# New prices per matrix product in the planner that orders TensorE's work in a hybrid decoder step

## The chip, the cores and the metric

One core of one Trainium2 chip. The metric is the device time of one execution in microseconds (us); lower is better. The comparison is of medians over several executions.

## The reference

Two layers of a hybrid decoder, on a prompt of 1024 tokens and on 8 single-token samples with cached state. Each layer projects the normalised input once and feeds three branches, whose gated outputs are joined and projected back:

```python
h = _rmsnorm(x, p['norm_g'], NORM_EPS)
z = h @ p['w_in']
u, g_pool, q, k, v, g_attn, rin, g_rwkv = _split(z, (D_POOL, D_POOL, D_ATTN, D_KV, D_KV, D_ATTN, D_SHIFT, D_RWKV))
a_out, new_pool = _pool_mixer(u, pool_buf, pos0, p['pool_w'], p['pool_scale'])   # windows of 2, 4, 8, 16 tokens
b_out, new_k, new_v = ...      # sliding-window attention (128), rotary, learned sinks
c_out, new_shift, new_wkv = _rwkv_mix(rin, shift_prev, wkv0, p)                  # a recurrence over tokens
mix = jnp.concatenate([a_out * silu(g_pool), b_out * silu(g_attn), c_out * silu(g_rwkv)], axis=-1)
y = x + mix @ p['w_out']
```

The recurrence is the part with a long chain in it; for each token it reads and updates a 64x64 state per head:

```python
sa = jnp.einsum('bhvk,bhk->bhv', S, kk_t)
S = S * w_t[:, :, None, :] - sa[..., None] * (kk_t * a_t)[:, :, None, :] + v_t[..., None] * k_t[:, :, None, :]
o = jnp.einsum('bhvk,bhk->bhv', S, r_t)
```

## The kernel before

**The work.** Tokens lie along the columns: two halves of 520 and 512, the first with the 8 samples in it. A layer's half is `in_half` (21 tiles of 128 output columns of `w_in`) and later `out_half` (8 tiles of `w_out`). Each operand of a projection is split into a high and a low part in a rounded 32-bit type (`hh`, `hl` for the activations, `wh`, `wl` for the weights) and three products are added, wh·hh, wh·hl and wl·hh, over 8 blocks of 128 rows. So a tile is 24 products of 512 columns, or 48 of 256 and 264. These are called products here; they all write a tile named `acc`. Every other matrix multiplication is in plain float32 and is small:

- `rwkv_prep` makes the terms of 256 tokens (a group g, four per layer): `lora`, `kn`, `bonus` twice, then `gram` twice; then a triangular solve on VectorE, then `CA<-cst,xrkv` and `CA<-cst,BK`.
- `rwkv_chain` runs the recurrence over 8 pieces of 32 tokens. A piece is three groups on TensorE, each waiting for the copies of the one before by VectorE and ScalarE: `CA<-XS,AG` (copied into `ys`), `CA<-ys,TZ` (copied into `XS`), `CA<-XS,BT` (copied into `XS` of the next piece). Outputs of the piece before (`CB<-XS,AG`) ride behind the first. After the last piece comes a group norm on `osb` (VectorE and ScalarE), then `back`, 16 small multiplications that turn `osb` around.
- attention: `ps` (scores), softmax, `pt` (transposes), `po` (values). Others: `qn`, `pn`, `pool`, `ssum`, `vtr`.

**What sets the order on TensorE.** The instructions of TensorE stand in one fixed order, chained by `placed` (line 289 on). It is worked out while the program is built, by a planner with a clock of its own, `pe[0]`, in us. Each multiplication adds its price in cycles, divided by 2400 (`pe[0] += cost / 2400.0`). The prices are in `mm` (from line 302) and `transpose`. Products are the background. After each of them `tick` looks at six streams of side work (chain, finishing steps, preparation, three of attention) and runs every step that has come due. When a step is due is worked out in `after`:

```python
least, scale = (MT0, MT1) if job.tight else (job.stream.least, job.stream.scale)
return pe[0] + scale * (at_of(*what) - pe[0]) + least
```

`at_of` is when the planner believes that the step's inputs are ready, from prices of the other engines' instructions. So delays are in us, and how many products lie in such a delay depends on what a product is priced at. Where the products have run out and a job must be finished, `need` moves the clock forward to the next step that comes due, and nothing lies between the steps then.

**The end.** `out_last` does the last half of layer 1. First it runs the products of 6 of the 8 row blocks, 8 tiles of 18 products of 512 columns, with the last chain between them (chain g = 3). Then it needs that chain, with `back` and two steps after it on POOL, and runs the 48 products of the last two row blocks. The orders of the other engines come from the framework's scheduler, which is given TensorE's.

Of the kernel before, what the change touches and what calls it, by code (L numbers as in the profile page):

```python
# [9 lines left out]
F32 = mybir.dt.float32  # L10
# [76 lines left out]
def hybrid_step_kernel(ctx: ExitStack, tc: tile.TileContext, I, O):  # L87
# [17 lines left out]
    def there(ap, at):  # L105
        name = ap.tensor.name
        ready[name] = max(at, ready.get(name, 0.0))
# [183 lines left out]
    def placed(ins, cost, out):  # L291
        if pe[1] is not None:
            tc.add_manual_dep(
                ins.ins, pe[1].name,
                mybir.DependencyInfo(mybir.DependencyClass.NoSync, mybir.DependencyReason.DATA),
                reason="order of the streams",
            )
        pe[1] = ins.ins
        pe[0] += cost / 2400.0
        there(out, pe[0] + 0.1)  # L300

    def mm(out, lhsT, rhs, start=True, stop=True, **kw):
        n = out.free_size()
        if rhs.dtype == F32:
            m = out.shape[0]
            half = m > 64 and lhsT.shape[0] <= 64
            n = max((2.7 if half else 4.2) * n, 500) if m > 64 else max(2.7 * n, 235) if m > 32 else max(1.6 * n + 64, 140)
        else:
            n = max(n, 270)
        placed(T.matmul(out=out, lhsT=lhsT, rhs=rhs, start=start, stop=stop, **kw), n, out)  # L310

    def transpose(out, in_, identity):
# [2 lines left out]
    def flip(out, in_, rows):  # L315

        mm(out=out, lhsT=in_, rhs=ident[rows, rows], start=True, stop=True)
# [68 lines left out]
    def products(w, xs, o, n, acc, k, of=8):  # L386
        wh, wl = w[k // 4]
        xh, xl = xs[0][k]
        for i, (a, b) in enumerate(((wh, xh), (wh, xl), (wl, xh))):
            mm(  # L390
                out=acc[:, :n], lhsT=a[:, k % 4, :], rhs=b[:, o:o + n],
                start=(k == 0 and i == 0), stop=(k == of - 1 and i == 2), skip_group_check=True,
            )
            tick()

    def products_wa(w, xs, o, n, acc, k):
        xh, xl = xs[0][k]
        wk = w[k // 4]
        mm(
            out=acc[:, :n], lhsT=wk[:, k % 4, :], rhs=xh[:, o:o + n], start=(k == 0), stop=(k == 7),  # L400
            skip_group_check=True,
        )
        tick()
        mm(
            out=acc[0:64, :n], lhsT=wk[:, k % 4, 0:64], rhs=xl[:, o:o + n], start=False, stop=(k == 7),
            skip_group_check=True,
        )
        tick()
# [1270 lines left out]
```

## Time and profile before

| | |
|---|---|
| median of 3 runs | 1204.05 us (1202.91 to 1211.36) |
| the profiled execution | 1207.17 us |
| its span, first to last instruction | 1205.4 us |
| TensorE (PE) busy, share of the span | 1100.6 us, 91% |
| VectorE (DVE), ScalarE (ACT), GpSimd (POOL) busy | 876.1, 620.8, 519.0 us |
| mean granted clock of TensorE | 0.953 of full |

A busy TensorE is one with a multiplication in flight. Multiplications are pipelined, so one of them lasts longer than the distance between two starts; that distance, from row to row of a timeline, is what one costs in a stream. A float32 multiplication is two records in the trace, one of the rounded type a single one. The granted clock is 1 at 2.4 GHz and 0.5 at 1.2 GHz.

### The profile page before, as it was taken

Reading aid. Unit: us, or ns where it says so; the run is one execution under the profiler, and the core shown is the slowest. Engines: PE = TensorE matmul, PEld = TensorE weight load, DVE = VectorE, ACT = ScalarE, POOL = GpSimd, SP = SyncE. Lnnn points to the kernel's source line nnn. Section 1 sums busy time; section 2 is a strip of 40 time slices with the busy share of each in tenths; the row PEclk is TensorE's granted clock in tenths of the full one; section 3 lists DMA queues with packets and bytes.
Section 4 is the critical chain, followed back from the end, with each engine's and each line's share of the span. In section 5 each row is a group of like instructions: output and inputs, shape, how many; then the busy total and the mean of one; then the engine's idle time right before and its main releaser. Section 6 shows DMA issues by size and latency. Waiting matters only on the chain.

```text
span 1205.4 us, 24519 instructions
## 1 busy us (share of the span) xinstructions
PE 1100.6 (91%) x9258; PEld 875.0 (73%) x9258; DVE 876.1 (73%) x1783; ACT 620.8 (52%) x1579; POOL 519.0 (43%) x544
## 2 busy tenths in 40 slices
PE   5999889899999898999999879999998889899995
PEld 4998778566766577878998768667676666688764
DVE  6548897668677885877788998896428796787523
ACT  4445454655546563655465536545645444655331
POOL 5156545433455245340364363444445534432441
PEclk8999999799999898999999999999999988999997
DMA  5442224322322134343422322443442121333221
GB/s 172 130 132 79 61 88 125 122 81 99 97 83 72 42 98 124 107 125 112 145 70 73 93 66 63 134 140 112 144 138 81 60 84 50 100 122 118 92 84 73
DMA packets 81234, 120.33 MB, mean 100 GB/s; under 512 B 20430, under 2 KB 30174, under 8 KB 81116
## 3 DMA queue, kind: packets, MB, share of 16 engines
q1 hardware_dynamic: 81116, 118.77, 31.6%
q8 instruction: 72, 1.18, 0.4%
q14 instruction: 46, 0.38, 0.1%
HBM read 94.28 MB, written 19.17 MB: 94 GB/s over the span
## 4 chain that ended last, share of the span: by engine, by line
PE 51%; DVE 30%; DMA 5%; issue 5%; ACT 5%; POOL 3%; SPq 2%; DVEq 0%; POOLq 0%; ACTq 0%
PE acc L310 35%; DVE pr L150 4%; PE CA L310 4%; DVE AG L150 3%; DVE hl L150 2%; PE po L310 2%; PE ps L310 2%; SPq L160 2%; DVE sm L150 2%; DVE X L150 2%; PE CB L310 2%; PE qn L310 1%; DVE pd L150 1%; DMA sq<-z 1%; DVE z L150 1%
## 5 line engine op out<-in xcount | busy, mean ns | idle before, releaser
L310 PE MATMUL acc<-hh,wh 128*128 128x512 f32 (+2 forms) x1464 | 496.7, 339 | 17.0 <-ACT hh L150 8.8
L310 PE MATMUL acc<-hh,wl 128*128 128x512 f32 (+2 forms) x1464 | 492.4, 338 | 11.8 <-POOL wl L150 8.5
L310 PE MATMUL acc<-hl,wh 128*128 128x256 f32 (+3 forms) x1464 | 494.5, 338 | 7.4 <-DVE hl L150 7.2
L150 POOL TENSOR_TENSOR wl<-wst,wh 128x512 fp32r<-128x512 f32 (+1 forms) x223 | 300.8, 1351 | 380.9 <-ACT wh L150 339.9
L310 PEld LDWEIGHTS acc<-hh,wh 128*128 128x128 f32 x1464 | 283.9, 194 | 56.2 <-issue 13.5
L310 PEld LDWEIGHTS acc<-hh,wl 128*128 128x128 f32 x1464 | 283.4, 194 | 47.3 <-POOL wl L150 11.6
L310 PEld LDWEIGHTS acc<-hl,wh 128*128 128x128 f32 (+1 forms) x1464 | 282.0, 193 | 45.5 <-DVE hl L150 12.2
L150 ACT CAST wh<-wst 128x512 fp32r<-128x512 f32 (+1 forms) x246 | 149.1, 607 | 158.3 <-PE acc L310 103.1
L150 DVE TENSOR_TENSOR pr<-X,N 128x4 f32<-128x4 f32 (+15 forms) x128 | 69.4, 542 | 5.0 <-POOL N L150 1.7
L150 ACT ACTIVATE sm<-sm,asm 128x129 f32<-128x129 f32 (+1 forms) x130 | 50.7, 392 | 18.4 <-DVE asm L150 16.9
L150 ACT ACTIVATE e<-e 128x520 f32<-128x520 f32 (+1 forms) x64 | 40.5, 633 | 30.5 <-DVE e L150 29.9
L310 PE MATMUL ps<-kh,q 64*128 64x256 f32 (+1 forms) x256 | 42.7, 424 | 11.0 <-DVE sm L150 6.6
L150 ACT COPY XS<-CB 32x128 f32<-32x128 f32 (+2 forms) x88 | 27.2, 309 | 43.2 <-PE CB L310 42.6
L150 DVE TENSOR_REDUCE X<-pr 128x2 f32<-128x4 f32 (+15 forms) x128 | 44.7, 349 | 2.3
L150 DVE SCALAR_TENSOR_TENSOR hl<-xh,vec,hh 128x520 fp32r<-128x520 f32 (+1 forms) x32 | 30.1, 949 | 20.0 <-ACT hh L150 19.6
L150 POOL TENSOR_TENSOR mx<-mx,e 128x520 f32<-128x520 f32 (+1 forms) x24 | 33.6, 1400 | 24.5 <-ACT e L150 16.3
L150 ACT ACTIVATE XS<-CB,pc 64x64 f32<-64x64 f32 x112 | 28.6, 303 | 25.4 <-PE CB L310 24.4
L150 POOL TENSOR_TENSOR z<-z,rope 128x520 f32<-128x520 f32 (+1 forms) x20 | 32.9, 1645 | 19.8 <-DMA sq<-z 15.1
L310 PEld LDWEIGHTS ps<-kh,q 64*128 64x128 f32 x256 | 25.9, 203 | 21.3 <-DVE sm L150 7.4
L150 DVE COPY XS<-CA 32x128 f32<-32x128 f32 (+1 forms) x72 | 20.7, 287 | 27.2 <-PE CB L310 24.7
L150 DVE TENSOR_TENSOR xr<-acc,xr 128x256 f32<-128x256 f32 (+2 forms) x48 | 24.5, 511 | 21.5 <-PE acc L310 21.0
L150 POOL COPY zs<-ev 128x9 f32<-128x9 f32 (+3 forms) x28 | 10.4, 370 | 66.0 <-DVE ev L150 65.2
(250 smaller groups left out, 1950.1 us busy)
## 6 DMA issues: line engine op xcount, KB each, us to landing
wst<-in_w_in_dram SPq DMA_DIRECT2D x175, 256.0 KB, 2.7
wst<-in_w_out_dram SPq DMA_DIRECT2D x56, 256.0 KB, 2.7
zr<-mz SPq DMA_DIRECT2D x24, 256.0 KB, 2.7
xrkv<-zr SPq DMA_DIRECT2D x16, 384.0 KB, 3.7
sq<-z SPq DMA_DIRECT2D x40, 65.0 KB, 2.0
sq<-z SPq DMA_DIRECT2D x40, 64.0 KB, 2.0
xh<-in_x_dram SPq DMA_DIRECT2D x8, 260.0 KB, 6.3
xr<-in_x_dram SPq DMA_DIRECT2D x8, 260.0 KB, 3.4
```

Source lines behind the costliest of these rows:

```text
L150: return f(*a, **kw)
L160: return nc.sync.dma_start(out, in_)
L310: placed(T.matmul(out=out, lhsT=lhsT, rhs=rhs, start=start, stop=stop, **kw), n, out)
```

## The change

It replaces four numbers in `mm` and adds one flag. Prices are in cycles of 2.4 GHz. n is the number of columns and m the number of output rows; `half` marks multiplications over 64 rows or fewer with more than 64 output rows (`ps`).

- A product cost max(n, 270): 270, 270 and 512 for 256, 264 and 512 columns. It now costs 1.1 n: 281.6, 290.4 and 563.2.
- A float32 multiplication with more than 64 output rows over all 128 rows cost 4.2 n and now costs 2.5 n; `half` goes from 2.7 n to 2.9 n; smaller ones keep their price.
- The first float32 multiplication after a rounded one costs 240 more.

```diff
+    turned = [False]
+
     def mm(out, lhsT, rhs, start=True, stop=True, **kw):
         n = out.free_size()
         if rhs.dtype == F32:
             m = out.shape[0]
             half = m > 64 and lhsT.shape[0] <= 64
-            n = max((2.7 if half else 4.2) * n, 500) if m > 64 else max(2.7 * n, 235) if m > 32 else max(1.6 * n + 64, 140)
+            n = max((2.9 if half else 2.5) * n, 500) if m > 64 else max(2.7 * n, 235) if m > 32 else max(1.6 * n + 64, 140)
+            if turned[0]:
+                n += 240
         else:
-            n = max(n, 270)
+            n = 1.1 * n
+
+        turned[0] = rhs.dtype != F32
         placed(T.matmul(out=out, lhsT=lhsT, rhs=rhs, start=start, stop=stop, **kw), n, out)
```

No instruction is added or removed. Their order changes on every engine. All lines behind `mm` stand six lower, so line 310 is line 316 now.

**The end of the last chain, on TensorE.** Before, from the last two products of the 6 blocks (`acc`) on: the last one and two thirds pieces of the chain, `back`, and the first of the 48 products.

```order
L310 MATMUL acc<-hl,wh 128x512
L310 MATMUL acc<-hh,wl 128x512
L310 MATMUL CA<-ys,TZ 32x64 x2
L310 MATMUL CB<-ys,TZ 32x64 x2
L310 MATMUL CA<-XS,BT 64x64 x2
L310 MATMUL CB<-XS,BT 64x64 x2
L310 MATMUL CA<-XS,AG 32x64 x4
L310 MATMUL CB<-XS,AG 32x64 x4
L310 MATMUL CA<-ys,TZ 32x64 x2
L310 MATMUL CB<-ys,TZ 32x64 x2
L310 MATMUL CA<-XS,BT 64x64 x2
L310 MATMUL CB<-XS,BT 64x64 x2
```

Behind these stand `CB<-XS,AG 32x64 x4` and at once `back`. Now, the same last step of the chain (`CA<-XS,BT`) with its last outputs (`CB<-XS,AG`):

```order
L316 MATMUL CA<-XS,BT 64x64 x2
L316 MATMUL CB<-XS,BT 64x64 x2
L316 MATMUL acc<-hl,wh 128x512
L316 MATMUL acc<-hh,wl 128x512
L316 MATMUL acc<-hh,wh 128x512
L316 MATMUL acc<-hl,wh 128x512
L316 MATMUL acc<-hh,wl 128x512
L316 MATMUL acc<-hh,wh 128x512
L316 MATMUL acc<-hl,wh 128x512
L316 MATMUL acc<-hh,wl 128x512
```

Three more products, the outputs and 32 products follow, then `back` and the 48. The six bare groups of before have products around them now, and 32 products stand between the last outputs and `back`.

**The third group of layer 1, on TensorE.** Before, around `back` of the chain before it (its `osb` comes from DVE), where `qn` is a row sum of the queries:

```order
L310 MATMUL acc<-hh,wh 128x512
L310 MATMUL acc<-hl,wh 128x512
L310 MATMUL back<-cst,osb 64x64 x16
L310 MATMUL acc<-hh,wl 128x512
L310 MATMUL acc<-hh,wh 128x512
L310 MATMUL qn<-sq,cst 128x512
L310 MATMUL acc<-hl,wh 128x512
```

Ten more products, the second `bonus`, 10 products, the first `gram`, 11 products and the second `gram` follow. Now, from the first `gram`:

```order
L316 MATMUL gram<-AG,BK 64x64 x16
L316 MATMUL acc<-hl,wh 128x512
L316 MATMUL qn<-sq,cst 128x512
L316 MATMUL acc<-hh,wl 128x512
L316 MATMUL acc<-hh,wh 128x512
L316 MATMUL acc<-hl,wh 128x512
L316 MATMUL acc<-hh,wl 128x512
L316 MATMUL acc<-hh,wh 128x512
L316 MATMUL acc<-hl,wh 128x512
L316 MATMUL back<-cst,osb 64x64 x16
```

Twenty products stand between the second `bonus` and this `gram`, and five between this `back` and the second `gram`. `back` has moved behind both `bonus` and the first `gram`, and the second `gram` from 21 products behind `bonus` to 32.

## Rows read from the trace of the kernel before

**Rows 1.** Head of the page: busy time, share of the span and instructions of each engine
```profile
span 1205.4 us, 24519 instructions
PE 1100.6 (91%) x9258; PEld 875.0 (73%) x9258; DVE 876.1 (73%) x1783; ACT 620.8 (52%) x1579; POOL 519.0 (43%) x544
```

**Rows 2.** Waits of TensorE: who for whom, us in total, times, longest
```profile
PE acc L310 <- ACT hh L150: 11.3, 4, 5.3
PE CA L310 <- DVE XS L150: 10.0, 13, 2.1
PE back L310 <- DVE osb L150: 8.8, 3, 4.8
PE gram L310 <- DVE AG L150: 7.5, 3, 4.3
PE CA L310 <- DVE ys L150: 5.2, 6, 1.5
```

**Rows 3.** Timeline of TensorE, the end: start, us, what, [idle before, releaser]
```profile
1172.85 0.39 PE L310 MATMUL acc<-hh,wl 128*128 128x512 f32 x1
1173.17 0.24 PE L310 MATMUL CA<-ys,TZ 128*32 128x64 f32 x1
...
1174.34 0.27 PE L310 MATMUL CA<-XS,BT 128*64 128x64 f32 x1 [0.75 <-DVE XS L150]
...
1177.71 0.32 PE L310 MATMUL CB<-XS,AG 128*32 128x64 f32 x8 [0.35 <-ACT XS L150]
1182.84 1.97 PE L310 MATMUL back<-cst,osb 64*64 64x64 f32 x32 [4.82 <-DVE osb L150]
1188.29 0.80 PE L310 MATMUL acc<-hh,wh 128*128 128x512 f32 x1 [3.47 <-ACT hh L150]
```

**Rows 4.** Timeline of TensorE, a chain group between products of 512 columns
```profile
1156.82 0.40 PE L310 MATMUL acc<-hl,wh 128*128 128x512 f32 x1
1157.15 0.32 PE L310 MATMUL CA<-XS,AG 128*32 128x64 f32 x8
...
1157.51 0.50 PE L310 MATMUL acc<-hh,wl 128*128 128x512 f32 x1
1157.85 0.39 PE L310 MATMUL acc<-hh,wh 128*128 128x512 f32 x1
1158.07 0.40 PE L310 MATMUL acc<-hl,wh 128*128 128x512 f32 x1
```

**Rows 5.** Timeline of TensorE, a float32 multiplication on the whole array between products
```profile
98.70 0.28 PE L310 MATMUL acc<-hh,wh 128*128 128x256 f32 x1
98.82 0.59 PE L310 MATMUL bonus<-rk,cst 128*128 128x256 f32 x2
99.06 0.47 PE L310 MATMUL acc<-hl,wh 128*128 128x256 f32 x1
99.37 0.27 PE L310 MATMUL acc<-hh,wl 128*128 128x256 f32 x1
```

**Rows 6.** Timeline of TensorE, the third group of layer 1
```profile
932.27 1.51 PE L310 MATMUL back<-cst,osb 64*64 64x64 f32 x32 [3.24 <-DVE osb L150]
...
941.77 1.15 PE L310 MATMUL gram<-AG,BK 64*64 64x64 f32 x32
949.96 1.97 PE L310 MATMUL gram<-AG,BK 64*64 64x64 f32 x32 [4.29 <-DVE AG L150]
```

**Rows 7.** Timelines of DVE and POOL: a group norm's last step, twice, and POOL beside it
```profile
930.53 1.68 DVE L150 TENSOR_TENSOR osb<-osb,gsm 128x512 f32<-128x512 f32 x1
1182.00 0.69 DVE L150 TENSOR_TENSOR osb<-osb,gsm 128x512 f32<-128x512 f32 x1 [0.61 <-ACT gsm L150]
...
930.03 1.64 POOL L150 TENSOR_TENSOR wl<-wst,wh 128x512 fp32r<-128x512 f32 x1
```

**Rows 8.** Stretches: us, then PE, PEld, DVE, ACT, POOL busy, granted clock, DMA share, GB/s
```profile
1150.00:1173.20 23.20, 23.20 (x177) 16.24 (x176) 5.06 (x13) 7.46 (x22) 9.38 (x9) 1.00 0.27 83
...
1188.30:1192.30 4.00, 4.00 (x9) 2.91 (x10) 2.04 (x3) 0.62 (x1) 0.00 (x0) 0.50 0.00 0
```

## The prediction

> **What bounds the kernel.** I read the page first, then the waits, then timelines of the places where a wait is long. TensorE is busy for 1100.6 of 1205.4 us [rows 1]. The change removes no multiplication, so it can only move the 104.8 us in which TensorE has nothing in flight, and the clock that goes with them. The other engines have slack as a sum, but not at each moment: the waits of TensorE name DVE and ACT [rows 2]. What counts is how much TensorE work stands between a group and the next one that needs its result. I call that the fill. Where the fill is shorter than the answer of DVE and ACT, TensorE stops, and all that is queued behind it stops as well, since its order is fixed.
>
> **What the new prices do to the order.** Due times are in us of the planner's clock. A product of 512 columns goes from 512 to 563.2 cycles, one of 264 from 270 to 290.4, one of 256 from 270 to 281.6. So a given delay holds 9, 7 and 4% fewer products. That squeezes all side work towards earlier products, and it ends earlier against the products that are there to cover it. Are the prices nearer to the trace? Two products of 512 start 0.23 us apart (1157.85 to 1158.07) [rows 4], which at 2.4 GHz is some 540 cycles; the new 563 is 4% over, the old 512 was 5% under. For 256 columns the 0.12 us from 98.70 to the next start [rows 5] are some 285 cycles, where the new price fits. The chain's groups: in [rows 4] the first product after 1156.82 would start at 1157.05, the third at 1157.51; the third starts at 1158.07. So this group, which carries outputs, costs 0.56 us, or 1340 cycles; the plan had 8 x 166.4 = 1331 for it and has 1571 now. The two other steps of a piece, half as many multiplications, had 666 and 940 and have 906 and 1180. Float32 on the whole array goes the wrong way: `bonus` in [rows 5] moves the products behind it by 99.37 - 98.82 - 0.12 = 0.43 us, 1030 cycles. The old price was 1075, the new one is 640, or 880 with the turn. There are about a hundred of these against 4416 products, so the squeeze decides.
>
> **Term 1, the end.** Before, the products of the 6 blocks run out at 1173.08 (1172.85 + 0.23), and `back` starts at 1182.84 [rows 3]. In these 9.76 us TensorE does six chain groups, each with a bare wait, and then idles 4.82 us for the group norm. In the new order the six groups stand among products. Up to 1173.2 that stretch has 8 to 10 products between two groups, and TensorE is in flight for all of its 23.20 us [rows 8], so such a fill (8 x 0.23 = 1.8 us) covers a step. They then cost 6 x 0.56 = 3.4 us. Behind the last outputs stand 32 products, 7.4 us, where the group norm takes 1182.84 - 1177.71 = 5.1 us [rows 3]. So `back` need not wait, and 9.76 - 3.4 = 6.4 us go. What is late next is what follows `back`: two steps on POOL and the split of `hh`, 3.47 us of idle time, unchanged. There is also the clock: the eight products from 1188.29 ran at 0.50 [rows 8] and took 3.9 us instead of 1.8. With 4.82 us less idle ahead of them I count half of that as gained, 1.0. Term: -7.4, from -5 (one more wait in the six groups, clock unchanged) to -9.
>
> One thing speaks against it. The group norm's multiplication took 0.69 us at 1182.00 with POOL idle and 1.68 us at 930.53, while POOL made a `wl` from 930.03 to 931.67 [rows 7]. In the new order POOL still makes `wl` tiles in that stretch. Two such operations would add 2 x 0.99, which makes 7.1 us against 7.4 of fill: still covered, with nothing to spare. The Trainium skill has this as a rule (SBUF — State Buffer, Summary: rules for kernel authors): a DVE operation with two SBUF inputs and a GpSimd one that reads SBUF exclude each other, and the second waits until the first is done. The trace agrees (DVE ends 0.54 us after POOL). By that rule, with all of the norm's operations behind a POOL one, term 1 would be about -6 instead of -7.4.
>
> **Term 2, the third group of layer 1.** `back` waits 3.24 us and the second `gram` 4.29 us, both for DVE [rows 6]. `gram` had 10 + 11 products behind its `bonus` (4.8 us) with another `gram` between; it now has 20 + 1 + 6 + 5 = 32 (7.4 us), with `qn`, `gram` and `back` between: `qn` of 512 columns is twice the 0.43 of `bonus`, 0.9, and `back` 1.5 [rows 6]. So it comes 2.5 + 0.9 + 1.5 = 4.9 us later, more than the wait. `back` had 42 products behind its chain and has 51, 2.1 us, with `bonus`, `gram` and `qn` besides (0.4, 1.2, 0.9) and four `lora` of 0.12 less: 4.1 us later, against 3.24. Term: -7.5, from 0 (DVE is late there in any case) to -11 with the clock.
>
> **Term 3, the chain elsewhere.** I counted the fill of the chain's 192 steps in both orders, with the starts of [rows 4, 5]. The middle value goes from 2.53 to 2.46 us (`AG` to `TZ`), from 2.69 to 2.46 (`TZ` to `BT`) and from 2.92 to 2.69 (`BT` to `AG`): on average 0.18 us less. The trace has 15.2 us of waits on `XS` and `ys` in 19 places [rows 2], 0.8 us each. Some 2 us and 4 places of that are bare steps of term 1. Fifteen waits longer by 0.18 us make 2.7, and a few steps that just made it are late by a little: I take +3, from 0 to +8 (one more step in ten short by 0.4 us).
>
> **Term 4, the other waits.** Of the 104.8 us, about 10 belong to term 1, 7.5 to term 2 and 13 to term 3. What is left is some 74 us: the start, where nothing can be hidden, the splits `hh` and `hl`, weights, attention. Their places move too. A long wait that goes in one place says little on new ones in another. With 4 to 9% less fill I take +6 (8% of 74), from -5 to +20.
>
> **Term 5, turns.** A run of tiled float32 groups costs more than its own columns. Such entries go from 274 to 276, all entries from a product or `lora` into float32 from 345 to 350. At no more than 0.2 us each this is +0.4 to +1.0; I take +0.7. The plan charges a turn by type, so that `bonus` pays one, but in [rows 5] it starts 0.12 us after the product ahead, as any product would, and its 0.43 us are its columns alone. The Trainium skill puts the cost elsewhere (TensorEngine Tiling, Key Properties): a change of tiling mode drains the engine, and a change of type is not mentioned. The trace agrees, and by that rule the term would be +0.4 instead of +1.0.
>
> **The sum.** -7.4 - 7.5 + 3 + 6 + 0.7 = -5.2. On the profiled execution, 1207.17, that gives 1202.0. It lies 3.1 us above the median of the runs, 1204.05, and from the median it gives 1198.9. I forecast 1199, 0.4% less.
>
> **Rivals.**
> - *A larger gain, 1186.* Terms 1 and 2 at their far ends (-9, -11), turns +0.7, term 3 at +1 and nothing new in term 4: -18. For it: the prices of products fit better, and the three long waits at the end and in the third group are answered by name. Against it: the waits lie in many places [rows 2], and those were found after the fact.
> - *No gain to speak of, 1206.* The plan does not do what it says: float32 on the whole array is now priced at two thirds of the trace, so the order is another one rather than a better one, and the 7.5 us of term 2 come back elsewhere. -7.4 + 3 + 6 + 0.7 = +2.3.
> - *Slower, 1219.* The chain is asked for too early. Its place is the 192 steps outside the end, its price a stop of everything behind it. If one step in four is short instead of one in ten, by 0.5 us, 13 us become 24, and the preparation and attention steps, squeezed by the same percentages, lose as much again: +22 to +23, less 7.4 at the end. It decides from the point at which the added waits exceed 15 us, that is the gains of terms 1 and 2. For it: DVE's answers vary, as the same operation at 0.69 and 1.68 us shows [rows 7]. Against it: the stretch before 1173 with 8 products per step shows no wait at all [rows 8].
>
> **Chances and range.** The forecast (1192 to 1204) 0.42, the larger gain 0.25, no gain 0.19, slower 0.14. A measurement of this kernel tells about 1% from no change (its three runs span 0.7%); 1% is 1192 and 1216. Faster by over 1%: 0.27, the larger gain and a little of the forecast; within 1%: 0.59; slower: 0.14. The range of 8 in 10 goes from 1182, a little beyond the larger gain, to 1218, where the slower case begins to be left out.
>
> **What would show it.** Right: in the timeline of the end, chain groups between products up to the last outputs, `back` with no wait on `osb`, and the 3.47 us on `hh` still there; `gram` and `back` of layer 1's third group without long waits; waits on `XS` and `ys` up by a few us. Wrong: TensorE's waits as a sum above 110 us; a wait of some us before `back` at the end, with POOL beside the group norm; or a busy time of TensorE that has grown, which no step here contains.

## The result, and the profile after

The changed kernel took 1222.44 us (median of 4 runs, 1216.03 to 1227.61) against 1203.48 us before: a ratio of 1.0141, with a 95% interval from 1.0105 to 1.0178. It is slower by 1.4%, outside the range, on the side that I had given 14%. The profiled execution took 1216.03 us and is the fastest of the four. Here and below, a ratio leaves out executions that took over 1.5% longer than the fastest of their kernel, which makes a difference only in e5.

The head of its page, with the busy time of each engine, as in [rows 1]:

```profile
span 1214.2 us, 24493 instructions
PE 1099.8 (91%) x9258; PEld 876.5 (72%) x9258; DVE 871.3 (72%) x1783; ACT 617.8 (51%) x1579; POOL 515.6 (42%) x544
```

TensorE is busy for the same time in these two executions (1099.8 against 1100.6), as no step removes or adds work. Its idle time went from 104.8 to 114.4 us, over the 110 that I had named as a sign of being wrong. So what this pair shows is lost in waits. But it shows only a part: its spans are 8.8 us apart, the medians 19.0. The mean granted clock of the four executions of the changed kernel is 0.958 (the profiled one), 0.955, 0.948 and 0.946; that of the profiled one of before is 0.953. The waits of TensorE, beside [rows 2]:

```profile
PE CA L316 <- DVE XS L150: 11.5, 12, 4.7
PE acc L316 <- ACT hh L150: 10.8, 4, 5.4
PE pool L316 <- DVE pd L150: 9.6, 2, 5.5
PE ps L316 <- DVE sm L150: 9.0, 7, 5.0
...
PE ps L316 <- DVE pr L150: 5.3, 2, 3.8
...
PE gram L316 <- DVE AG L150: 4.6, 3, 3.2
...
PE pt L319 <- DVE so L150: 4.0, 2, 2.2
...
PE vtr L319 <- DVE z L150: 3.2, 3, 2.2
PE CA L316 <- DVE ys L150: 2.8, 3, 1.0
...
PE back L316 <- DVE osb L150: 0.2, 1, 0.2
```

`back` waited 8.8 us for `osb` before and now 0.2. `gram` went from 7.5 to 4.6. The chain (`XS` and `ys`) waits 14.3 instead of 15.2. What is new are waits of the finishing steps and of attention. These are the rows that before had for some of them:

```profile
PE ps L310 <- DVE sm L150: 6.6, 2, 4.5
...
PE pool L310 <- DVE pd L150: 3.3, 2, 3.0
...
PE ps L310 <- DVE pr L150: 0.6, 1, 0.6
```

`pool` on `pd` went from 3.3 to 9.6 us, `ps` from 6.6 and 0.6 to 9.0 and 5.3, and `pt` on `so` and `vtr` on `z` have no row before.

The end, in the timeline of TensorE, beside [rows 3]: the last outputs of the chain, the last product of the 6 blocks, `back`, and the first of the 48 products.

```profile
1183.19 0.32 PE L316 MATMUL CB<-XS,AG 128*32 128x64 f32 x8
...
1190.78 0.39 PE L316 MATMUL acc<-hh,wl 128*128 128x512 f32 x1
1191.10 1.15 PE L316 MATMUL back<-cst,osb 64*64 64x64 f32 x32
1196.46 0.80 PE L316 MATMUL acc<-hh,wh 128*128 128x512 f32 x1 [4.22 <-ACT hh L150]
```

`back` starts where the product ahead of it leaves off. From the last product of the 6 blocks to the first of the 48 it is 5.7 us now and was 15.4 (1172.85 to 1188.29). Some of the difference is chain groups that stand earlier now. The products come in the same order in both kernels, so the two traces can be laid side by side by the number of the product: the 4320th of 4416 starts 20.3 us later than before, the last one only 8.4 us later. The end did gain, and the body (all that lies ahead of the end) lost. Of the 20.3 us, 15.2 are more idle time; in the rest TensorE did side work that came later before. The body did not fall behind evenly: 4.1 us at product 600, 15.8 at product 1800, 14.0 at product 3120, 20.3 at product 4320, so nothing was lost between 1800 and 3120.

The third group of layer 1, beside [rows 6]:

```profile
951.62 1.15 PE L316 MATMUL gram<-AG,BK 64*64 64x64 f32 x32
953.70 1.12 PE L316 MATMUL qn<-sq,cst 128*128 128x512 f32 x2 [0.51 <-ACT sq L150]
958.74 1.97 PE L316 MATMUL back<-cst,osb 64*64 64x64 f32 x32 [2.53 <-DVE AG L150]
```

The two waits of 3.24 and 4.29 us are gone (the second `gram` now stands at 962.63, with no wait). But `back` now stands behind the first `gram`. They write the one buffer of the `rw` pool in turn, so `back` waits 2.53 us until DVE has read `gram` into `AG`.

And one of the new waits, for the pooling of layer 1's first half. TensorE first, then the DVE instructions ahead of it:

```profile
732.35 2.10 PE L316 MATMUL pool<-pd,pw 128*128 128x256 f32 x4 [5.45 <-DVE pd L150]
```

```profile
729.99 0.29 DVE L150 SCALAR_TENSOR_TENSOR pd<-pd,pst 64x8 f32<-64x8 f32 x1
730.20 0.17 DVE L150 TENSOR_TENSOR pd<-pb,cst 64x15 f32<-64x15 f32 x1
730.28 0.67 DVE L150 SCALAR_TENSOR_TENSOR pd<-pb,u 64x497 f32<-64x497 f32 x1
730.98 0.17 DVE L150 TENSOR_TENSOR pd<-pd,u 64x15 f32<-64x15 f32 x1
731.07 0.42 DVE L150 TENSOR_TENSOR mx<-acc,ss 128x264 f32<-128x264 f32 x1
731.41 0.67 DVE L150 TENSOR_TENSOR ss<-ss,pr 128x512 f32<-128x512 f32 x1
732.12 0.17 DVE L150 TENSOR_TENSOR pd<-pd,u 64x15 f32<-64x15 f32 x1
```

The last 0.17 us of `pd` stand behind an evacuation (`mx`) and a step of the samples (`ss`). DVE has no pause here; it does other streams' work between the steps of this one. Nothing in the prices of products speaks of that.

### The profile page after: what moved, and what is told of

Its sections match the earlier page's. It is cut to its first block, busy times and chain, and to the rows that moved or that the text cites. A ratio compares the mean times of both kernels' runs of the same rounds, so it can differ in the third digit from the quotient of the medians.

```text
span 1214.2 us, 24493 instructions
## 1 busy us (share of the span) xinstructions
PE 1099.8 (91%) x9258; PEld 876.5 (72%) x9258; DVE 871.3 (72%) x1783; ACT 617.8 (51%) x1579; POOL 515.6 (42%) x544
## 5 line engine op out<-in xcount | busy, mean ns | idle before, releaser
L150 DVE TENSOR_TENSOR pr<-X,N 128x4 f32<-128x4 f32 (+15 forms) x128 | 72.1, 564 | 5.6 <-POOL N L150 2.7
L316 PE MATMUL ps<-kh,q 64*128 64x256 f32 (+1 forms) x256 | 45.5, 417 | 14.7 <-DVE sm L150 9.0
```

The costliest lines, as they stand in the source:

```text
L150: return f(*a, **kw)
```

## The experiments

The theory after the result was the one I had written as a rival: dearer products leave less fill, so TensorE asks too early (**squeeze**). Its rivals were that the bad prices of float32 on the whole array spoil the plan (**small prices**, later **pair**), and that the order is what counts, whichever way prices move (**lottery**). Lottery was first written as "any other order loses some 5 to 20 us"; from e6 on it is a draw that can lose or gain, and its ranges are so wide that meeting them shows little. All ratios are to the kernel before, run on the same chip.

**e1, the price of the products alone.**

```diff
-            n = max(n, 270)
+            n = 1.1 * n
```

> The kernel before with the new price of the products alone (1.1 n); float32 keeps its old prices and there is no turn. Theory squeeze (the loss of the change comes from products that are priced dearer, so that a delay holds fewer of them): the body loses what it lost in the whole change, the end gains as much as there, so 1215 to 1228 us. Rival lottery (the old order fits the chip because its numbers were set on it; any other order loses some 5 to 20 us in the body, whichever way the prices move): anything from 1200 to 1225, no clear tie to the whole change. Rival small prices (float32 on the whole array is now far too cheap): 1192 to 1200, since the bad prices are gone and the gain at the end stays.

Measured: 1195.39 us, ratio 0.9937 (0.9912 to 0.9962). This plan has the products' full price and is faster. Squeeze had said 1215 at least, and lottery 1200 at least: both miss. Small prices meets its 1192 to 1200.

**e2, the prices of float32 alone.**

```diff
-            n = max((2.7 if half else 4.2) * n, 500) if m > 64 else ...
+            n = max((2.9 if half else 2.5) * n, 500) if m > 64 else ...
```

> The kernel before with the new prices of float32 alone (2.5 n and 2.9 n), products as before, no turn. Squeeze: products are not dearer, so no loss in the body, and the end keeps part of its bare chain: 1200 to 1206. Lottery: the order is another one, so 1207 to 1225. Small prices: 1212 to 1225, the loss of the whole change without its gain at the end.

Measured: 1192.58 us, ratio 0.9908 (0.988 to 0.9935). The prices that contradict the trace make the better plan here. Small prices, which had said 1212 at least, falls; but squeeze (1200 to 1206) and lottery (1207 to 1225) miss as well.

**e3, the turn alone.**

```diff
+            if turned[0]:
+                n += 240
...
+        turned[0] = rhs.dtype != F32
```

> The kernel before with the 240 cycles of a turn alone. Squeeze: a side step that costs more takes planner time from the products as well, so a part of the loss, 1204 to 1212. Lottery: 1207 to 1225. Small prices: 1200 to 1206, since nothing is priced too cheap by it.

Measured: 1206.01 us, ratio 1.0034 (1.0007 to 1.006). It fits squeeze as well as small prices, and lies just under lottery's lower end.

**e4, a change that says nothing.**

```diff
-            n = max(n, 270)
+            n = max(n, 268)
```

> The kernel before with the floor of a product's price at 268 cycles in place of 270, a change of 0.7% that says nothing. Squeeze and small prices: 1200 to 1207, the same as before within the measurement. Lottery: a new order like any other, so 1207 to 1225.

Measured: 1208.83 us, ratio 1.0048 (1.002 to 1.0077). A 0.7% change of one price moves the time by half a per cent. Nor do the parts add up to the change: 0.9937, 0.9908 and 1.0034 multiply to 0.988, where the change measured 1.0141.

**e5, the end alone.**

```diff
-            n = max(n, 270)
+            n = (1.3 if late[0] else 1.0) * max(n, 270)
...
+    late[0] = True
     out_half(1, 0, split_mix(0, m10))
```

> The kernel before with its old prices up to the second half of layer 1's input projections, and from the output projection of layer 1's first half on a product priced 1.3 times as high, so that the last chain ends 33 products before those of the 6 blocks do. It is term 1 alone: everything ahead of that point stands in the old order. Term 1 as predicted: 1204 - 7.4 = 1196 to 1197 us. If the end is worth what the end of the changed kernel shows against before (20.3 us behind at product 4320, 8.4 at the last one): 1192. Rival (the end is hidden by something else, the writes or the steps on POOL): 1202 to 1206.

Measured: ratio 0.9957 (0.9919 to 0.9996), that is -5.2 us, from seven of its twelve executions. The median of all twelve is 1205.79 us against 1205.63 before: no gain, and inside the rival's 1202 to 1206. So the times alone do not show the gain, and the trace has to. In its timeline `back` follows the last outputs at a distance that covers the group norm, and the wait for `hh` stays:

```profile
1167.79 0.24 PE L312 MATMUL CB<-XS,AG 128*32 128x64 f32 x4
1175.83 1.15 PE L312 MATMUL back<-cst,osb 64*64 64x64 f32 x32
1182.81 0.79 PE L312 MATMUL acc<-hh,wh 128*128 128x512 f32 x1 [4.00 <-ACT hh L150]
```

The products again come in the same order as before. At product 3841, the first behind the point where the two orders part, e5 is 2.2 us ahead of before; at the last one it is 5.7 ahead. In this pair the end is worth 3.5 us, less than the 5 that term 1 had as its small end.

**e6, the change without the turn.**

```diff
-            if turned[0]:
-                n += 240
```

> The changed kernel without the 240 cycles of a turn: products and float32 at their new prices. Alone they gave 0.9937 and 0.9908. Additive theory (each price has its own effect): 0.985, 1186 us, and the turn then has to be worth +2.9% beside them where it was +0.3% alone. Lottery theory (each set of prices draws another order, and the sum of two effects says nothing): anywhere from 1190 to 1225.

Measured: 1214.12 us, ratio 1.0085 (1.0058 to 1.0111). The products' price and the float32 price gain 0.6% and 0.9% apart and lose 0.85% together, so in the times the effects of the parts do not add up.

**e7, the new order up to layer 1's first output projection, old prices behind it.**

```diff
-            n = 1.1 * n
+            n = 1.1 * n if not late[0] else max(n, 270)
```

(and the same for the two other prices)

> The changed kernel with the old prices back from the output projection of layer 1's first half on; up to there it stands in the new order, and the last chain ends 10 products before those of the 6 blocks instead of 32. If the loss lies in the body: 1222 plus up to 5, so 1220 to 1228 us. If it lies in the end, where I counted a gain: 1204 to 1212.

Measured: 1230.18 us, ratio 1.0198 (1.0157 to 1.0238). The loss is in the body, as the side by side of the products had it (the time is a little above the 1220 to 1228 that this reading had said). The end of the changed kernel is worth 1230.18 - 1222.44 = 7.7 us against this one, 6.9 by the ratios, and 5.8 in the two traces from product 3841 on.

**e8, the change with 1.09 n.**

```diff
-            n = 1.1 * n
+            n = 1.09 * n
```

> The changed kernel with 1.09 n instead of 1.1 n for a product, a change of 0.9% that says nothing. Lottery: a new draw from the same urn, so 1190 to 1215, nearer to the four others of this kind (1193 to 1209) than to 1222. Systematic theory (these three prices together make a bad plan): 1217 to 1227.

Measured: 1213.17 us, ratio 1.0069 (1.004 to 1.0098). Half of the loss goes with a change that says nothing, but it stays slower than before. The idle time of the body (see below) is the same 104.8 us in both profiles; the granted clock is not, on average 0.960 here and 0.952 in the change.

**e9, the products alone with 1.105 n.**

```diff
-            n = 1.1 * n
+            n = 1.105 * n
```

(in the kernel of e1)

> The new price of the products alone, as in e1, but 1.105 n instead of 1.1 n. Theory that the price of products has an effect of its own (e1's 0.9937): 1193 to 1199 us again. Lottery: this plan leaves four steps of the last chain bare where e1 has 40 products behind the chain, so the gain at the end is gone, and the body is a new draw: 1203 to 1220.

Measured: 1204.96 us, ratio 0.9981 (0.9958 to 1.0004). A product that is 0.5% dearer than in e1 gives a plan whose last chain is bare again, and e1's gain is gone. So the covered end, too, is no steady effect of dearer products: it came with 1.1 n and not with 1.105 n. The two bodies are much alike (94.6 and 93.3 us of idle time up to product 3841, see below); behind it e9 has 7.1 us more.

**e10, the change with delays 8% longer.**

```diff
-MC0 = 1.14
-MC1 = 1.46
+MC0 = 1.2312
+MC1 = 1.5768
```

(and the other nine constants likewise)

> The changed kernel with every delay of the plan (least and scale of each stream, the group norm's) 8% longer, so that as many products lie in a delay as before the change; 23 products stay behind the last chain. Squeeze: the loss of the body goes, the gain at the end stays, 1195 to 1201 us. Lottery: a new draw, 1198 to 1222, with waits in other places.

Measured: 1215.37 us, ratio 1.0077 (1.0054 to 1.01). About as many products lie in a delay as before the change, and the loss of the body stays; squeeze had said 1195 to 1201. So the longer delays did not undo it. But it is one plan, whose order is new as well.

**e11, float32 prices and the turn, products as before.**

> The new prices of float32 and the turn, the products as before. Alone the two gave 0.9908 and 1.0034. Additive: 0.994, 1197 us. Lottery: 1193 to 1222, no tie to that.

Measured: 1201.65 us, ratio 0.9952 (0.9928 to 0.9976), near the 0.994 of adding the parts. One sum that fits among those that don't.

**e12, float32 prices of e2 with the end of e5.**

> The new prices of float32 alone (the fastest so far, 1192.6 us), and from the output projection of layer 1's first half on a product priced 1.3 times as high, which puts 31 products behind the last chain where e2 left its last steps bare. All ahead of that point stands in e2's order. If the end is a cause of its own (e5: about -5), it adds to e2: 1186 to 1189. If not: 1191 to 1195.

Measured: 1185.41 us, ratio 0.9826 (0.9798 to 0.9854), 7.2 us below e2, and 9.9 by the ratios (before took 1206.70 us beside e12 and 1203.98 beside e2). From product 3841 on its trace gains 8.0 us on that of e2. It beats both kernels. Its head, and the waits at its end:

```profile
span 1181.8 us, 24509 instructions
PE 1088.1 (92%) x9258; PEld 869.7 (74%) x9258; DVE 860.1 (73%) x1783; ACT 619.7 (52%) x1579; POOL 516.8 (44%) x544
```

```profile
1166.42 0.49 PE L315 MATMUL acc<-hh,wh 128*128 128x512 f32 x1 [0.39 <-ACT hh L150]
1167.55 0.50 PE L315 MATMUL acc<-hl,wh 128*128 128x512 f32 x1 [0.64 <-DVE hl L150]
```

`back` and the steps after it are covered as well, so of the 3.47 us of [rows 3] for `hh` 0.39 are left. The end is a cause of its own: it gains on this body, on that of before (e5, by less) and on that of the change (against e7).

What was open then: all five plans with both new prices were slower than before, the others lay between 0.9826 and 1.0048. Was that pair bad as a rule?

**e13, products at 1.1 n with 2.5 n on the whole array; scores at their old price.**

```diff
-            n = max((2.9 if half else 2.5) * n, 500) if m > 64 else ...
+            n = max((2.7 if half else 2.5) * n, 500) if m > 64 else ...
```

(in the kernel of e6)

> Products at 1.1 n and float32 on the whole array at 2.5 n; the scores keep 2.7 n, no turn. Theory pair (the loss is made by dear products together with float32 on the whole array priced at two thirds of what the trace shows): 1212 to 1220 us, like e6. Lottery: a new draw, 1190 to 1222, as likely below 1208 as above.

Measured: 1224.14 us, ratio 1.0144 (1.0108 to 1.0179). It is slow as the pair theory had it, and above its 1212 to 1220.

**e14, products at 1.1 n with scores at 2.9 n; the whole array at its old price** (`2.9 if half else 4.2` in the kernel of e6).

> Products at 1.1 n and the scores at 2.9 n; float32 on the whole array keeps 4.2 n, no turn. Theory pair with the whole array as the culprit: 1193 to 1203 us, like e1 and e9. If the scores' price is the culprit: 1212 to 1220. Lottery: 1190 to 1222.

Measured: 1222.17 us, ratio 1.0139 (1.0105 to 1.0174). Without the price that is wrong by the trace it is just as slow, where the theory with that price as the culprit had said 1193 to 1203.

**e15, e6 with 2.55 n in place of 2.5 n.**

```diff
-            n = max((2.9 if half else 2.5) * n, 500) if m > 64 else ...
+            n = max((2.9 if half else 2.55) * n, 500) if m > 64 else ...
```

> e6 (products at 1.1 n, scores at 2.9 n, no turn) with float32 on the whole array at 2.55 n instead of 2.5 n, a change of 2% that says nothing. Theory pair: 1210 to 1218 us once more. Lottery: a new draw, as likely below 1208 as above.

Measured: 1193.11 us, ratio 0.9898 (0.9867 to 0.993). The pair is still there, one price has moved by 2%, and the time by 1.9%, from slower than before to faster. As a rule, the pair theory falls. The heads and the clock of e6 and e15:

```profile
span 1206.3 us, 24511 instructions
PE 1093.1 (91%) x9258; PEld 874.9 (73%) x9258; DVE 871.6 (72%) x1783; ACT 619.4 (51%) x1579; POOL 518.4 (43%) x544
...
core 0: 1206.3 us, clock 0.953
```

```profile
span 1191.7 us, 24513 instructions
PE 1086.2 (91%) x9258; PEld 867.6 (73%) x9258; DVE 867.7 (73%) x1783; ACT 619.2 (52%) x1579; POOL 518.4 (43%) x544
...
core 0: 1191.7 us, clock 0.963
```

Idle time falls from 113.2 to 105.5 us, and the clock rises from 0.953 to 0.963.

**e16, all prices by the trace.**

```diff
-            n = max((2.9 if half else 2.5) * n, 500) if m > 64 else ...
-            if turned[0]:
+            n = max((2.9 if half else 4.05) * n, 500) if m > 64 else ...
+            if turned[0] and (half or m <= 64 or lhsT.shape[0] <= 64):
```

> The changed kernel with float32 on the whole array at 4.05 n, as its starts in the trace of before have it, and the turn's 240 cycles only ahead of groups that use a part of the array. All prices are then nearer to the trace than before or after. Theory pair: the bad price is gone, 1193 to 1203 us. Theory that a plan gets better with truer prices: below 1195. Lottery: 1190 to 1222.

Measured: 1220.92 us, ratio 1.0121 (1.0082 to 1.016). Its end is covered like that of the change, and its waits lie elsewhere once more. In the waits of before, the three groups shown here have 7.5, 0.4 and 1.3 us:

```profile
PE gram L316 <- DVE AG L150: 13.4, 4, 5.8
...
PE po L316 <- DVE sm L150: 8.7, 6, 4.1
PE ssum L316 <- DVE pr L150: 6.4, 2, 5.8
```

Truer prices did not make a better plan here. The prices of the other engines' work, and the order in which DVE takes the streams, are not in them.

**What orders the plans.** Sixteen new bodies or ends lie between 0.9826 and 1.0198 of before, with no price that decides the sign. What does follow is where the time goes. Over the 18 profiles a straight line fits the span: 1059 us, and 1.01 for each us of TensorE's idle time (span less busy), and 0.34 for each us at the lower clock (2 x span x (1 - mean clock), since a rate of 0.5 loses half). It leaves 3.5 us of scatter out of 11.8. (That idle time counts about once is no surprise, as the span is busy and idle time; what the line adds is the price of the clock.) Before: 104.8 idle and 113 at the lower clock; after: 114.4 and 102; e15: 105.5 and 88; e12: 93.7 and 83.

One price does leave a mark, which shows best ahead of the end. Product 3841 is the first of layer 1's `out_half`, the point at which e5, e7 and e12 switch prices. Here are the stretches up to it, in before, e5, the change, e7, e4 and e15:

```profile
0.00:1044.92 1044.92, 958.84 (x7904) 761.40 (x7905) 783.21 (x1585) 556.51 (x1402) 464.65 (x491) 0.95 0.32 100
0.00:1042.72 1042.72, 954.29 (x7904) 760.38 (x7905) 785.55 (x1585) 555.65 (x1401) 463.77 (x491) 0.96 0.32 100
0.00:1070.53 1070.53, 965.75 (x8032) 768.07 (x8032) 796.74 (x1619) 563.64 (x1428) 466.80 (x494) 0.96 0.32 99
0.00:1079.98 1079.98, 974.41 (x8033) 774.74 (x8033) 804.50 (x1619) 564.06 (x1428) 464.62 (x494) 0.94 0.31 98
0.00:1044.17 1044.17, 950.18 (x7904) 759.16 (x7905) 780.64 (x1585) 553.04 (x1400) 466.92 (x490) 0.96 0.31 100
0.00:1037.79 1037.79, 947.04 (x7944) 755.61 (x7945) 784.86 (x1603) 561.37 (x1420) 467.97 (x493) 0.96 0.32 101
```

Length less PE busy is TensorE's idle time in the body. It repeats where the order is the same: 86.1 us before and 88.4 in e5, 104.8 in the change and 105.6 in e7. The four other bodies with products at or near their old price (e2, e3, e4, e11) have 84.3 to 94.0 us, the ten with products at 1.09 n or more 90.7 to 105.6: on average 3.7 and 14.0 us more than before. So dearer products do tilt the body towards waits, though the two groups overlap (e4 has 94.0, e15 90.7 and e9 93.3). Squeeze was right in this direction. In the whole time the same two groups average 0.9986 and 1.0059. How the price does it is open: e10, with the longer delays, still has 99.3 us.

## Why the prediction was wrong

**Term 1, the end (-7.4), held in its mechanism, and roughly in its size.** Three pairs give it: by the ratios e5 against before -5.2, e12 against e2 -9.9, the change against e7 -6.9; in the traces, from where the orders part, -3.5, -8.0 and -5.8. `back` does not wait, and the wait for `hh` stays late next, as said (3.47 to 4.22). POOL did lengthen the norm's last multiplication, once (1.44 us at 1188.11, beside a `wl` from 1187.71 to 1189.00), but did not uncover it: it ends 1.55 us before `back`, and outputs to `back` is 7.9 us. The 1.0 us for the clock did not come: the first eight of the 48 products take 3.88 us in both traces, at a granted clock of 0.50.

**Term 2, the third group (-7.5), came out at -5.0.** The two waits went, but I had not seen that `back`, once behind the first `gram`, needs the buffer that DVE has yet to read. The order that I quoted shows the two in a row.

**Term 3, the chain elsewhere (+3), came out at +0.7.** Waits on `XS` and `ys` went from 15.2 to 14.3; without the bare steps of the end, which are not in this term, from 13.6 to 14.3. Less fill by 0.18 us mattered little to these waits.

**Term 4, the other waits (+6, from -5 to +20), is the step that failed.** Idle time rose by 9.6 us although the end freed 10.2 - 4.2 = 6.0 and the third group 5.0. The chain took 0.7. So the rest took some 9.6 + 6.0 + 5.0 - 0.7 = 20 us, the far end of what I allowed, where I had +6. I had taken it as a squeeze of what was there, by 8%. What was there is not kept: waits of the old order went, and others grew (`pool`, `ps`) or came that it did not have (`pt`, `vtr`). I had seen that long waits that go say little on new ones, and still counted the ones that go by name at -7.5 and the ones that come by a percentage. The direction was right: dearer products tilt the body towards waits, on average by some 10 us more than other new prices do. Which step of the planner carries it, and how much of the 20 us is the draw of this order, stays open.

**The clock has no term outside the end.** The terms above are idle time of the profiled pair, whose spans are 8.8 us apart. The other 10 us between the medians lie in executions of which no trace is kept. Their granted clock is on record: 0.952 as the mean of the four, against 0.959 for the 101 executions of before beside the experiments. That is 118 and 99 us at the lower clock, where the profiled pair had 102 and 113. By the line's 0.34 for each us, (19 + 11) x 0.34 = 10 us of the loss would be the clock's and not in the pair; that is an estimate.

**Term 5, turns,** +0.7, is too small to be seen.

**The rivals.** The slower one had the sign and, at 1219, nearly the time, but that is in part luck. The first half of its mechanism, the chain asked too early (+11), is not what happened: the chain took 0.7. Its second half, waits of preparation and attention (+11), is where the time went, at about twice the size. And its sum left out the -7.5 of term 2 and the clock. That "the order is another one rather than a better one" was written as a case without gain. It is the better part of the right reading: e4, e8, e9 and e15 show that a price moved by 0.5 to 2% draws another order that is up to 1.9% off. Against such a scatter the chances were too narrow: 0.14 for slower by over 1%, where 5 of the 15 plans that reorder the body are (the change, e7, e13, e14 and e16; e5 and e12, which only add an end to another plan's body, are left out), and one, e15, is faster by as much. All five have dearer products, but so has e15.

## What to carry to other kernels

A static order from a planner is to a large part a draw: before crediting or blaming a new price, move it by a per cent that means nothing and see what that does; only an effect that stands above this scatter, or that adds to several different orders as the covered end does here, is an effect. Look for places where a chain must be bare (no background left) and give the planner a reason to end it earlier there, without touching the order elsewhere; that was worth some 0.3 to 0.8% by itself and, on the better draw, 1.7% against the kernel before. Where several draws are at hand, compare them in the stage that a price acts on, by idle time: two executions of one order agreed there within about 2 us, and a tilt showed that no single time did. When counting waits, price those that a new order adds from the total of the old one, not from the few that it removes by name.

## What was not expected of the hardware

The time at the lower clock goes with a large part of the scatter between executions of one program. Before has 113 us of it in its profiled execution. Single executions of it, taken beside e9, went from 1199.58 us at a mean granted clock of 0.964 to 1212.75 us at 0.953. And the same DVE step is unsteady. The step of the pooling that makes `pb` from `pa` took 1.79 us in one place and 0.70 in another of the profiled execution of the changed kernel, with the same shape:

```profile
718.25 1.79 DVE L150 TENSOR_TENSOR pb<-pa 128x525 f32<-128x525 f32 x1
...
411.12 0.70 DVE L150 TENSOR_TENSOR pb<-pa 128x525 f32<-128x525 f32 x1
```

As in [rows 7], POOL lies beside the slow one, with two `wl` from 717.90 on:

```profile
717.90 3.28 POOL L150 TENSOR_TENSOR wl<-wst,wh 128x512 fp32r<-128x512 f32 x2 [2.83 <-ACT wh L150]
```

Over this whole execution it is regular: five of the twelve `pb<-pa` begin while POOL is making a `wl`; they take 1.38 to 1.79 us and end 0.55 to 0.57 us after that `wl` does. The other seven take 0.68 to 0.71 us. A planner with one price per element cannot see this.
